# Norm1's row spread by full products, its load on ScalarE's queue, and k's first cast behind h's: the prologue of an encoder block on one core

## The chip, the core and the metric

The kernel runs on one NeuronCore of a Trainium2 chip. The metric is the device time of one execution in microseconds (us). Before the change it is 890.23 us, the median of three runs (890.15, 890.23 and 893.89).

## The reference

One layer of a bidirectional encoder over x of 512 tokens by 1024 channels, all in float32. Cut to what matters here:

```python
h = rmsnorm(x, norm1_w[l])          # y = x * rsqrt(mean(x*x) + eps) * norm1_w
proj = h @ w_in[l]                  # pooling | q | k | v | z | betas, decays | merge gates
# branch A: multi-scale pooling; branch B: conv + SiLU + l2norm on q/k/v, gated delta rule
# forward and backward, gated RMSNorm; merge; output projection; residual
h2 = rmsnorm(x, norm2_w[l])
u = dwconv_centered(h2 @ ffn_up[l], ffn_conv_w[l], ffn_conv_b[l])
x = x + (silu(gate) * val) @ ffn_down[l]
return rmsnorm(x, final_norm_w)
```

The change concerns the first line, `rmsnorm(x, norm1_w)`, and the first two products with `w_in`: the 32 columns of betas and decays (`gate`) and the first 128 columns of k (`k0`).

## The kernel before, in words

Every float32 product with a weight is done as three fp32r products of high and low parts: `mm3` (L370 to L373) multiplies high by high, high by low and low by high. A weight block of 128 columns is loaded by SyncE's queue, its high part is a ScalarE cast (L392), its low part two subtractions on GpSimd (POOL, L396), each over half of the contraction. The activations h are stored transposed, as `h_hi` and `h_lo`.

The order of the work is set by a planner: each task is declared with its engine, an estimated cost, the buffers that it reads and writes and a key; `Planner.run` simulates the engines and, whenever one is free, takes the ready task with the smallest key. The program is then written out in that order, and every engine executes its own part of it in that order. A small key (-9e6) means early; `FEED` (-3e6) is the key of weight loads and casts.

The prologue before the change:

- POOL fills the constants one after another: the identity `ident`, eps tiles, the all-ones tile `ones`, triangular and mask tiles.
- TensorE (PE) does 13 and then 8 transposes of the identity (`pe_warm`, L571 to L574), whose result nobody reads.
- SyncE loads x in four tiles of 128 tokens (x0 to x3), and between x0 and x1 the row `norm1_w`, 1024 numbers in one partition (`load_n1`).
- `spread_n1` (L560 to L565) spreads that row over 128 partitions by two products of a 1x128 row of ones with 1x512 halves of the row, into two PSUM banks `n1b`.
- `norm_transpose` (L503 to L543) is done for each tile of 128 tokens: ScalarE sums the squares (L511) and takes the root (L514), VectorE (DVE) inverts it (L516) and scales the tile in two halves by the root and by `n1b` (L522), PE transposes each half in four 128x128 pieces (L533), ScalarE casts the result to `h_hi` (L537), DVE subtracts to `h_lo` (L541).
- The gate's products (L442 to L445) and k0's (`mm3`) are done in halves of 256 tokens, so that they can begin with x0 and x1.

Of the kernel before, what the change touches and what calls it, by code (L numbers as in the profile page):

```python
# [9 lines left out]
F32 = mybir.dt.float32  # L10
# [4 lines left out]
P = 128  # L15
S = 512
NT = S // P
D = 1024
# [19 lines left out]
class Planner:  # L38
# [14 lines left out]
    def add(self, eng, cost, fn, r=(), w=(), key=0.0, tab=None, kb=0.0, after=(), land=LAND):  # L53
        t = Task()
        t.land = land
        t.i, t.eng, t.cost, t.fn, t.key, t.tab, t.kb = len(self.tasks), eng, cost, fn, key, tab, kb
        t.preds, t.succs, t.news, t.uses = set(), [], [], set()
        for names, writes in ((r, False), (w, True)):
            for name in names:
                base = name.split("#")[0]  # L60
                known = self.parts.setdefault(base, {})
                ring = base.split(":")[0]
                if ring in self.rings and base not in t.news:
                    t.news.append(base)
                if base not in self.owner:
                    self.owner[base] = t.i
                    if ring in self.rings:
                        self.order[ring].append(base)
                t.uses.add(base)
                hit = list(known) if name == base else [n for n in (base, name) if n in known]  # L70
                for n in hit:
                    wr, rd = known[n]
                    if wr is not None:
                        t.preds.add(wr)
                    if writes:
                        t.preds.update(rd)
                if name == base and writes:
                    known.clear()
                wr, rd = known.get(name, (None, ()))
                known[name] = (t.i, ()) if writes else (wr, rd + (t.i,))  # L80
        t.preds.discard(t.i)
        for b in after:
            t.preds.update(self.users.get(b, ()))
        for b in t.uses:
            self.users.setdefault(b, []).append(t.i)
        self.tasks.append(t)
# [101 lines left out]
def ca(n):  # L188
    return 0.22 + n * 0.00082
# [6 lines left out]
def cp(n):  # L196
    return 0.17 + n * 0.0023
# [12 lines left out]
def hybrid_block(  # L210
# [23 lines left out]
    pe, act, dve, pool, sp = nc.tensor, nc.scalar, nc.vector, nc.gpsimd, nc.sync  # L234
# [16 lines left out]
    def with_table(tab, fn):  # L251
        def run():
            if table["now"] != tab:
                table["now"] = tab
                if TABLES[tab]:
                    act.preload_act_table_set(TABLES[tab])
            fn()

        return run

    def A(cost, fn, r=(), w=(), key=0.0, tab=None):
        add("act", cost, with_table(tab, fn) if tab else fn, r, w, key, tab)

    def V(cost, fn, r=(), w=(), key=0.0):
        add("dve", cost, fn, r, w, key)

    def G(cost, fn, r=(), w=(), key=0.0):
        add("pool", cost, fn, r, w, key)

    def M(cost, fn, r=(), w=(), key=0.0):  # L270
        add("pe", cost, fn, r, w, key)

    def L(kb, fn, r=(), w=(), key=0.0, after=(), land=Planner.LAND, issue=Planner.ISSUE, eng="sp"):
        add(eng, issue, fn, r, w, key, kb=kb, after=after, land=land)
# [6 lines left out]
    FEED, EVICT, CHAIN = -3e6, -2e6, -1e6  # L281

    def f32(ap):
        return ap.bitcast(F32)

    def bank(tag, name):
        return psum.tile([P, 512], F32, tag=tag, bufs=RINGS[tag], name=name)

    def banks2(name, shape=(P, 2, 512)):
        return psum.tile(list(shape), F32, tag="oo", bufs=RINGS["oo"], name=name)  # L290

    stacks = {}
    pools = {}
# [11 lines left out]
    ident = const.tile([P, P], F32, name="ident")  # L305
# [7 lines left out]
    qeps_t = const.tile([P, 1], F32, name="qeps_t")  # L313
    pool.memset(qeps_t, float(P) * EPS * L2_EPS)
    ones = const.tile([P, P], F32, name="ones")
    pool.memset(ones, 1.0)
    ones_r = const.tile([P, P], F32R, name="ones_r")
    tri = const.tile([P, 2, P], F32, name="tri")

# [40 lines left out]
    def ring(pool_name, tag, shape, dt, name):  # L360
        return pools[pool_name].tile(list(shape), dt, tag=tag, bufs=RINGS[tag], name=name)
# [15 lines left out]
    def next_unit():  # L377
        unit["n"] += 1
        return unit["n"] * 100.0

    def weights(src, kt, n, name, u):

        b = {}

        def load():
            b["raw"] = wpool.tile([P, kt, n], F32, tag="wraw", bufs=RINGS["raw"], name=f"wr_{name}")
            sp.dma_start(b["raw"], src)

        def hi():
            b["hi"] = wpool.tile([P, kt, n], F32R, tag="whi", bufs=RINGS["whi"], name=f"wh_{name}")  # L390
            b["lo"] = wpool.tile([P, kt, n], F32R, tag="wlo", bufs=RINGS["wlo"], name=f"wl_{name}")
            act.copy(b["hi"], b["raw"])  # L392

        def lo(i):
            sl = slice(i * kt // 2, (i + 1) * kt // 2)
            pool.tensor_tensor(out=b["lo"][:, sl], in0=b["raw"][:, sl], in1=f32(b["hi"][:, sl]), op=ALU.subtract)  # L396

        whi, wlo = f"whi:{name}", f"wlo:{name}"
        L(kt * n * P * 4 / 1024, load, w=[f"raw:{name}"], key=FEED + u)
        A(ca(kt * n), hi, r=[f"raw:{name}"], w=[whi, f"{wlo}#0"], key=FEED + u)  # L400
        for i in range(2):
            G(cp(kt * n / 2), lambda i=i: lo(i), r=[f"raw:{name}", whi], w=[f"{wlo}#{i}"], key=FEED + u)
        return b, whi, wlo

    def job(src, kt, xs, xr, name, halves=False, pair=False):
# [6 lines left out]
        if pair:  # L412
            def load():
                box["raw"] = wpool.tile([P, kt, n], F32, tag="wraw", bufs=RINGS["raw"], name=f"wr_{name}")
                sp.dma_start(box["raw"], src)

            def split():
                w = box["hi"] = wpool.tile([P, kt, 2 * n], F32R, tag="whi", bufs=RINGS["whi"], name=f"wp_{name}")
                act.copy(w[:, :, 0:n], box["raw"])

            def split2():
                w = box["hi"]
                pool.tensor_tensor(out=w[:, :, n:], in0=box["raw"], in1=f32(w[:, :, 0:n]), op=ALU.subtract)

            whi = f"whi:{name}"
            wlo = whi
            L(128, load, w=[f"raw:{name}"], key=FEED + u)
            A(ca(kt * n), split, r=[f"raw:{name}"], w=[whi], key=FEED + u)
            G(cp(kt * n), split2, r=[f"raw:{name}"], w=[whi], key=FEED + u)
        else:  # L430
            wb, whi, wlo = weights(src, kt, n, name, u)
# [121 lines left out]
    xin = [None] * NT  # L553
    n1 = {}

    def load_n1():
        n1["row"] = pools["st"].tile([1, D], F32, name="n1row")
        sp.dma_start(n1["row"], norm1_w)

    def spread_n1():  # L560
        n1["bc"] = banks2("n1b")
        for hf in range(2):
            pe.matmul(
                n1["bc"][:, hf, :], ones[0:1, :], n1["row"][:, hf * 512 : (hf + 1) * 512], start=True, stop=True
            )  # L565

    def load_x(t):
        xin[t] = pools["st"].tile([P, D], F32, name=f"x1_{t}")
        sp.dma_start(xin[t], xt[t * P : (t + 1) * P, :])

    def pe_warm(n):  # L571
        pt = bank("ds", f"pt_warm{n}")
        for i in range(n):
            pe.transpose(pt[:, 0:P], ident, ident)  # L574

    def hx(k):
        return h_hi[:, k, :], h_lo[:, k, :]
# [819 lines left out]
        L(256, lambda: sp.dma_start(g_scr["m1"][c], b["t"]), r=[f"y:lgp{c}"], w=[f"gscrm1{c}"], key=u - 300)  # L1397


    M(2.6, lambda: pe_warm(13), w=["ds:warm0"], key=-9e6)  # L1400
    A(1.3, lambda: act.preload_act_table_set("sqrt_and_others"), key=-9e6)
    for t, k in ((0, -9e6), (1, -8.9e6), (2, FEED + 240), (3, FEED + 250)):
        L(512, lambda t=t: load_x(t), w=[f"st:x{t}"], key=k)
    L(4, load_n1, w=["st:n1"], key=-8.95e6)
    M(2.0, spread_n1, r=["st:n1"], w=["oo:n1"], key=-8.9e6)
    M(1.6, lambda: pe_warm(8), w=["ds:warm1"], key=-8.8e6)
    for t in range(NT):
        norm_transpose(
            -8e6 + t, lambda t=t: xin[t], [f"st:x{t}"], lambda: [lambda: n1["bc"][:, 0, :], lambda: n1["bc"][:, 1, :]], ["oo:n1", "oo:n1"],
            lambda: h_hi, lambda: h_lo, "h", t,  # L1410
            lambda t=t: ring("st", "xs", (P, D), F32, f"xs_{t}"), f"xs:{t}", f"a{t}", None,
        )
# [108 lines left out]
    for t in range(NT):  # L1521
        L(512, lambda t=t: sp.dma_start(x2[t], xt[t * P : (t + 1) * P, :]), r=["pool:xp"], w=[f"xr{t}#0", f"xr{t}#1"],
          key=unit["n"] * 100, after=[f"pp:do{1 + t}"])
    L(512, lambda: sp.dma_start(pools["n2b"], norm2_w[0].partition_broadcast(P)), r=["pool:xp"], w=["n2b"],
      key=unit["n"] * 100, after=["pp:do5"])
# [48 lines left out]
    for i, (t, hf) in enumerate(order):  # L1574
        u = next_unit()
# [113 lines left out]
    for c in range(NF):  # L1689
        b = {}  # L1690
        for j in range(2):
            c0 = j * FFN + c * P
            box, pp, u = job(ffn_up[0][:, c0 : c0 + P], KD, hx2, hr2, f"up{c}_{j}", halves=c == 0)
# [273 lines left out]
```

## Time and profile before

| | |
|---|---|
| median of three runs | 890.23 us |
| the profiled execution, its own time | 891.73 us |
| span of the profiled execution | 890.0 us |
| busy: PE / PE's weight loads | 877.3 / 738.6 us |
| busy: DVE / ACT / POOL | 547.9 / 461.3 / 497.4 us |
| granted TensorE clock, mean of the run | 0.999 |

Read it from the top: one engine is busy almost throughout, the others are not; so the question for any change is whether it makes PE start earlier, wait less or do less. "PEld" is PE's weight load, which overlaps with its products. SP is SyncE, whose DMA queue carries most loads; ACT is ScalarE; POOL is GpSimd. A plain fp32 product appears as two records in the trace, a transpose as one.

### The profile page before, as it was taken

The page shows a single profiled execution, that of the slowest core. Times are in us where ns is not written, and L with a number is a line of the kernel's source. Part 1 is how long each engine was busy: PE and PEld are TensorE (multiplying, and loading weights), DVE is VectorE, ACT ScalarE, POOL GpSimd, SP SyncE. Part 2 cuts the span into 40 slices and gives each one's busy share as a digit, 9 for nine tenths or more (in the row PEclk, how much of TensorE's full clock was granted, in tenths as well). Part 3 has the DMA queues.
Part 4 walks back from the last instruction along what each step waited for, and adds up shares of the span by engine and source line. Part 5 has one row for each costly group of instructions (what it writes and reads, how often), then busy time and mean ns, then how long its engine had stood idle before and what let it go on. Part 6 is the DMA issues. An engine that isn't in the chain of part 4 may idle for free.

```text
span 890.0 us, 14085 instructions
## 1 busy us (share of the span) xinstructions
PE 877.3 (99%) x5178; PEld 738.6 (83%) x5178; DVE 547.9 (62%) x980; ACT 461.3 (52%) x791; POOL 497.4 (56%) x447
## 2 busy tenths in 40 slices
PE   8999999999999999999999999999999999999997
PEld 6988888798888887888788888888888888888886
DVE  4758686247795976654434243655655554569996
ACT  6589633417868344344844333444443333465664
POOL 3444455225366554253577905777878774567763
PEclk9999999999999999999999999999999999999999
DMA  7265448415255467112798605566766653366554
GB/s 203 78 208 143 124 119 185 102 37 142 60 166 131 119 167 119 31 48 83 250 312 266 193 20 202 200 216 217 240 214 201 234 167 98 116 192 199 167 170 161
DMA packets 176265, 140.20 MB, mean 158 GB/s; under 512 B 32110, under 2 KB 143547, under 8 KB 176196
## 3 DMA queue, kind: packets, MB, share of 16 engines
q1 hardware_dynamic: 167300, 137.20, 50.7%
q10 hardware_dynamic: 8896, 2.10, 1.6%
q8 instruction: 41, 0.67, 0.3%
q14 instruction: 28, 0.23, 0.1%
HBM read 114.08 MB, written 25.20 MB: 156 GB/s over the span
## 4 chain that ended last, share of the span: by engine, by line
PE 96%; DVE 2%; ACT 1%; issue 0%; POOL 0%; DVEq 0%; ACTq 0%; POOLq 0%
PE ps_up L372 9%; PE ps_up L373 9%; PE ps_up L371 9%; PE dn L371 4%; PE dn L372 4%; PE dn L373 4%; PE ps_k L371 2%; PE pw L1139 2%; PE o L1176 2%; PE ps_gp L371 2%; PE ps_k L372 2%; PE ps_k L373 2%; PE ps_wo L372 2%; PE ps_wo L371 2%; PE ps_wo L373 2%; PE ps_gp L372 2%
## 5 line engine op out<-in xcount | busy, mean ns | idle before, releaser
L396 POOL TENSOR_TENSOR wl_up<-wr_up,wh_up 128x512 fp32r<-128x512 f32 x88 | 114.2, 1319 | 53.2 <-ACT wh_up L392 51.0
L372 PE MATMUL ps_up<-h_lo,wh_up 128*128 128x512 f32 (+1 forms) x368 | 139.9, 380 | 0.3 <-DVE h_lo L541 0.3
L371 PE MATMUL ps_up<-h_hi,wh_up 128*128 128x512 f32 (+1 forms) x368 | 140.0, 380 | 0.0
L373 PE MATMUL ps_up<-h_hi,wl_up 128*128 128x512 f32 (+1 forms) x368 | 139.8, 380 | 0.0
L1680 DVE SCALAR_TENSOR_TENSOR c<-ps_up,fw,c 128x511 f32<-128x511 f32 x88 | 66.0, 750 | 101.6 <-ACT c L1674 99.8
L1665 POOL TENSOR_TENSOR tp<-tp 128x512 f32<-128x512 f32 x44 | 60.1, 1366 | 40.0 <-DMA tp<-in_ffn_down_dram 32.0
L1869 POOL TENSOR_TENSOR w_dn<-wr_dn,w_dn 128x512 fp32r<-128x512 f32 x44 | 65.5, 1503 | 29.1 <-ACT w_dn L1866 27.6
L372 PEld LDWEIGHTS ps_up<-h_lo,wh_up 128*128 128x128 f32 x368 | 69.2, 188 | 13.5 <-DVE h_lo L541 0.5
L371 PEld LDWEIGHTS ps_up<-h_hi,wh_up 128*128 128x128 f32 x368 | 69.2, 188 | 13.3
L373 PEld LDWEIGHTS ps_up<-h_hi,wl_up 128*128 128x128 f32 x368 | 69.2, 188 | 13.1
L392 ACT CAST wh_up<-wr_up 128x1024 fp32r<-128x1024 f32 x44 | 46.2, 1051 | 63.8 <-issue 25.5
L1866 ACT CAST w_dn<-wr_dn 128x512 fp32r<-128x512 f32 x69 | 42.4, 621 | 29.5 <-PE dn L373 21.1
L372 PE MATMUL dn<-w_dn,as 128*128 128x512 f32 x141 | 54.2, 385 | 0.0
L373 PE MATMUL dn<-w_dn,as 128*128 128x512 f32 x141 | 54.2, 385 | 0.0
L371 PE MATMUL dn<-w_dn,as 128*128 128x512 f32 x141 | 54.2, 385 | 0.0
L1634 DVE TENSOR_TENSOR as<-a,as 128x512 fp32r<-128x512 f32 (+1 forms) x41 | 42.8, 1069 | 0.1
L396 POOL TENSOR_TENSOR wl_k<-wr_k,wh_k 128x512 fp32r<-128x512 f32 x16 | 20.1, 1281 | 32.8 <-ACT wh_k L392 17.0
L1630 ACT CAST as<-a 128x512 fp32r<-128x512 f32 (+1 forms) x41 | 21.5, 534 | 32.3 <-DVE a L1701 28.6
L396 POOL TENSOR_TENSOR wl_v<-wr_v,wh_v 128x512 fp32r<-128x512 f32 x16 | 20.4, 1294 | 27.7 <-ACT wh_v L392 27.7
L1674 ACT ACTIVATE c<-ps_up,fw 128x512 f32<-128x512 f32 x44 | 33.9, 770 | 0.0
L396 POOL TENSOR_TENSOR wl_z<-wr_z,wh_z 128x512 fp32r<-128x512 f32 x16 | 20.4, 1295 | 22.8 <-ACT wh_z L392 22.8
L396 POOL TENSOR_TENSOR wl_gp<-wr_gp,wh_gp 128x512 fp32r<-128x512 f32 x16 | 21.5, 1364 | 19.6 <-ACT wh_gp L392 18.0
(361 smaller groups left out, 2438.2 us busy)
## 6 DMA issues: line engine op xcount, KB each, us to landing
wr_up<-in_ffn_up_dram SPq DMA_DIRECT2D x44, 512.0 KB, 3.8
tp<-in_ffn_down_dram SPq DMA_DIRECT2D x22, 512.0 KB, 5.2
t_scr<-tp SPq DMA_DIRECT2D x44, 256.0 KB, 2.5
wr_dn<-t_scr SPq DMA_DIRECT2D x20, 512.0 KB, 3.7
wr_dn<-in_ffn_down_dram SPq DMA_DIRECT2D x15, 512.0 KB, 3.6
x<-in_x_dram SPq DMA_DIRECT2D x8, 512.0 KB, 5.4
wr_k<-in_w_in_dram SPq DMA_DIRECT2D x8, 512.0 KB, 5.8
wr_z<-in_w_in_dram SPq DMA_DIRECT2D x8, 512.0 KB, 4.0
```

What stands on the lines that cost most here:

```text
L371: pe.matmul(ps, ahi, bhi, start=first, stop=False)
L372: pe.matmul(ps, ahi, blo, start=False, stop=False)
L373: pe.matmul(ps, alo, bhi, start=False, stop=last)
L392: act.copy(b["hi"], b["raw"])
L396: pool.tensor_tensor(out=b["lo"][:, sl], in0=b["raw"][:, sl], in1=f32(b["hi"][:, sl]), op=ALU.subtract)
L1630: act.copy(sets[p][:, i : i + n, 0, :], src())
L1634: dve.tensor_tensor(out=w[:, :, 1, :], in0=src(), in1=f32(w[:, :, 0, :]), op=ALU.subtract)
L1665: G(cp(512), lambda o=o, x=x, y=y: pool.tensor_tensor(out=w(*o), in0=w(*x), in1=w(*y), op=ALU.subtract), r=[n(*x), n(*y)], w=[n(*o)], key=u)
L1674: act.activation(b[j], box["ps"], AF.Identity, scale=fw[:, 1, ci : ci + 1], bias=fw[:, 3, ci : ci + 1])
L1680: dve.scalar_tensor_tensor(out=y[:, lo:hi], in0=box["ps"][:, lo + sh : hi + sh], scalar=fw[:, k, ci : ci + 1], in1=y[:, lo:hi], op0=ALU.mu ...
L1866: act.copy(b["w"][:, 0, :], raw["t"][:, j, :])
L1869: eng.tensor_tensor(out=b["w"][:, 1, :], in0=raw["t"][:, j, :], in1=f32(b["w"][:, 0, :]), op=ALU.subtract)
```

## The change

- `ones` is filled by VectorE instead of POOL.
- The row of norm1 gets a tile of 128 partitions that VectorE clears; the row is loaded into its first partition by ScalarE's queue, and the spread is a full product with the 128x128 tile of ones. The two halves are two tasks; their waits are declared apart.
- The warming is eight plain products of `ones` with itself, ahead of the spread, and three behind it, in place of 13 and 8 transposes ahead of it.
- k0's cast is declared to come behind the four casts of h of the first two token tiles, with a key among norm1's. The statistics of x2 are declared to come behind the two casts of x1's tile.

```diff
-    pool.memset(ones, 1.0)
+    dve.memset(ones, 1.0)
...
+        first = [f"h#hi{t}{hf}" for t in range(2) for hf in range(2)] if name == "k0" else []
-        A(ca(kt * n), hi, r=[f"raw:{name}"], w=[whi, f"{wlo}#0"], key=FEED + u)
+        A(ca(kt * n), hi, r=[f"raw:{name}", *first], w=[whi, f"{wlo}#0"], key=-8e6 + 1.5 if first else FEED + u)
...
+    def clear_n1():
+        n1["row"] = pools["st"].tile([P, D], F32, name="n1row")
+        dve.memset(n1["row"], 0.0)
+
     def load_n1():
-        n1["row"] = pools["st"].tile([1, D], F32, name="n1row")
-        sp.dma_start(n1["row"], norm1_w)
-
-    def spread_n1():
-        n1["bc"] = banks2("n1b")
-        for hf in range(2):
-            pe.matmul(
-                n1["bc"][:, hf, :], ones[0:1, :], n1["row"][:, hf * 512 : (hf + 1) * 512], start=True, stop=True
-            )
+        act.dma_start(n1["row"][0:1, :], norm1_w)
+
+    def spread_n1(hf):
+
+        if hf == 0:
+            n1["bc"] = banks2("n1b")
+        pe.matmul(n1["bc"][:, hf, :], ones, n1["row"][:, hf * 512 : (hf + 1) * 512], start=True, stop=True)
...
-            pe.transpose(pt[:, 0:P], ident, ident)
+            pe.matmul(pt[:, 0:P], ones, ones, start=True, stop=True)
...
-    M(2.6, lambda: pe_warm(13), w=["ds:warm0"], key=-9e6)
+    M(3.3, lambda: pe_warm(8), w=["ds:warm0"], key=-9e6)
...
-    L(4, load_n1, w=["st:n1"], key=-8.95e6)
-    M(2.0, spread_n1, r=["st:n1"], w=["oo:n1"], key=-8.9e6)
-    M(1.6, lambda: pe_warm(8), w=["ds:warm1"], key=-8.8e6)
+    V(0.6, clear_n1, w=["st:n1"], key=-9.5e6)
+    L(0, load_n1, w=["st:n1"], key=-8.95e6, eng="act")
+    for hf in range(2):
+        M(1.0, lambda hf=hf: spread_n1(hf), r=["st:n1"], w=[f"oo:n1#{hf}"], key=-8.9e6)
+    M(0.7, lambda: pe_warm(3), r=["oo:n1"], w=["ds:warm1"], key=-8.8e6)
     for t in range(NT):
         norm_transpose(
-            -8e6 + t, lambda t=t: xin[t], [f"st:x{t}"], lambda: [lambda: n1["bc"][:, 0, :], lambda: n1["bc"][:, 1, :]], ["oo:n1", "oo:n1"],
+            -8e6 + t, lambda t=t: xin[t], [f"st:x{t}", *(["h#hi10", "h#hi11"] if t == 2 else [])], lambda: [lambda: n1["bc"][:, 0, :], lambda: n1["bc"][:, 1, :]], ["oo:n1#0", "oo:n1#1"],
```

What stands in a row on PE, from the program's first product to the gate's first, before (the lines are those of the kernel before; `pt_warm` is the warming, `n1b` the spread row, `pt_a` a transposed half of x):

```order
L574 MATMUL pt_warm_156<-ident 128x128 x13
L574 MATMUL pt_warm_215<-ident 128x128 x8
L563 MATMUL n1b<-n1row,ones 128x512 x2
L533 MATMUL pt_a_0_256<-ident,xs_233 128x128 x4
L533 MATMUL pt_a_1_267<-ident,xs_233 128x128 x4
```

and now:

```order
L578 MATMUL pt_warm_156<-ones 128x128 x8
L569 MATMUL n1b<-n1row,ones 128x512 x2
L578 MATMUL pt_warm_231<-ones 128x128 x3
L535 MATMUL pt_a_0_245<-ident,xs_223 128x128 x4
L535 MATMUL pt_a_1_255<-ident,xs_223 128x128 x4
```

Ten products fewer stand ahead of the first transposes of x, and three of the warming ones have moved behind the spread.

ScalarE from its first instruction to the statistics of x2, before (`wp_gate` is the gate's weight, `wh_k` k0's high part, `h_hi` a cast of h, `xs_292` the square sum of x2):

```order
L1401 ACT_TABLE_LOAD
L1419 CAST ones_r<-ones 128x128
L511 ACTIVATE xs_233,nst_a_234<-x_0_171 128x1024
L514 ACTIVATE nst_a_234<-nst_a_234,eps_t 128x1
L511 ACTIVATE xs_245,nst_a_246<-x_1_201 128x1024
L514 ACTIVATE nst_a_246<-nst_a_246,eps_t 128x1
L419 CAST wp_gate<-wr_gate 128x8x32
L392 CAST wh_k_263<-wr_k_209 128x1024
L537 CAST h_hi<-pt_a_0_256 128x4x128
L537 CAST h_hi<-pt_a_1_267 128x4x128
L537 CAST h_hi<-pt_a_0_277 128x4x128
L511 ACTIVATE xs_292,nst_a_293<-x_2_213 128x1024
```

and now:

```order
L1405 ACT_TABLE_LOAD
L563 DMA n1row<-in_norm_w_dram 1x1024
L1425 CAST ones_r<-ones 128x128
...
L421 CAST wp_gate<-wr_gate 128x8x32
L539 CAST h_hi<-pt_a_0_245 128x4x128
L539 CAST h_hi<-pt_a_1_255 128x4x128
L539 CAST h_hi<-pt_a_0_265 128x4x128
L539 CAST h_hi<-pt_a_1_273 128x4x128
L392 CAST wh_k_280<-wr_k_201 128x1024
L513 ACTIVATE xs_291,nst_a_292<-x_2_207 128x1024
```

k0's cast has moved behind all four casts of h, x2's square sum behind both, and the row's load stands between the table load and the first cast.

On PE the gate's first half was cut by three groups of k0's products (`ps_k`); now it stands in one piece ahead of them:

```order
L444 MATMUL ps_gate<-h_hi,wp_gate 64x256
L445 MATMUL ps_gate<-h_lo,wp_gate 32x256 x2
L447 MATMUL ps_gate<-h_hi,wp_gate 64x256
L371 MATMUL ps_k_312<-h_hi,wh_k_280 128x256
L372 MATMUL ps_k_312<-h_lo,wh_k_280 128x256
L373 MATMUL ps_k_312<-h_hi,wl_k_281 128x256
```

The same 16 products of the gate and the same eight groups of k0 stand ahead of the gate's second half, in another order. From there on the rows of every engine are those of before.

## Rows read from the trace of the kernel before

**Rows 1.** The page of the profile: busy time, share of the span and instructions of each engine, and the engines' shares of the chain of work that ended last.

```profile
PE 877.3 (99%) x5178; PEld 738.6 (83%) x5178; DVE 547.9 (62%) x980; ACT 461.3 (52%) x791; POOL 497.4 (56%) x447
...
PE 96%; DVE 2%; ACT 1%; issue 0%; POOL 0%; DVEq 0%; ACTq 0%; POOLq 0%
```

**Rows 2.** The table by stretches, its first three: the stretch and its length in us, busy us (and instructions) of PE, PEld, DVE, ACT and POOL, granted TensorE clock, share of the DMA engines, GB/s.

```profile
0.00:12.50 12.50, 9.94 (x32) 7.03 (x33) 2.51 (x6) 6.13 (x11) 6.93 (x52) 1.00 0.92 273
12.50:25.00 12.50, 12.17 (x96) 11.23 (x95) 8.62 (x15) 8.00 (x19) 1.50 (x3) 1.00 0.38 94
25.00:50.00 25.00, 25.00 (x154) 22.04 (x153) 17.42 (x38) 17.14 (x38) 11.55 (x10) 1.00 0.32 88
```

**Rows 3.** Whom PE waited for in the whole span: us in total, times, longest.

```profile
PE l1a L962 <- ACT nm L1028: 1.4, 1, 1.4
PE pt_v L778 <- ACT cv_v L763: 1.3, 1, 1.3
```

**Rows 4.** The chain of work that ended last, from 0 to 30 us, in order of time: start us, us, what.

```profile
6.37 3.72 PE n1b L563 x4
...
10.12 0.76 DVE xs L522
...
11.01 2.81 PE pt_a L533 x12
...
15.20 0.31 PE ps_gate L443
15.51 0.11 PE ps_gate L442
15.62 0.12 PE ps_gate L443
...
18.54 0.44 PE pt_a L533 x4
...
22.33 0.12 PE ps_gate L442
...
27.05 1.01 PE pt_gate L607 x8
```

**Rows 5.** The timeline from 0 to 26 us: start us, us, engine, line, operation, out<-in, count, and in brackets the idle time before and what ended it.

```profile
0.80 1.28 ACT L1401 ACT_TABLE_LOAD   x1 [0.80 <-PEq L1954]
...
1.04 0.20 POOL L316 MEMSET ones<- 128x128 f32 x1
1.26 0.32 SPq L558 DMA_DIRECT2D n1row<-in_norm_w_dram  x1
...
1.63 4.74 PE L574 MATMUL pt_warm<-ident 128*128 128x128 f32 x21 [1.63 <-POOL ident masks.py:199]
...
4.44 1.06 ACT L511 ACTIVATE xs<-x 128x1024 f32<-128x1024 f32 x1 [2.05 <-DMA x<-in_x_dram]
...
5.95 0.16 DVE L516 RECIPROCAL nst_a<-nst_a 128x1 f32<-128x1 f32 x1 [5.95 <-ACT nst_a L514]
...
8.42 1.04 ACT L392 CAST wh_k<-wr_k 128x1024 fp32r<-128x1024 f32 x1 [0.77 <-DMA wr_k<-in_w_in_dram]
9.54 2.49 POOL L396 TENSOR_TENSOR wl_k<-wr_k,wh_k 128x512 fp32r<-128x512 f32 x2 [1.09 <-ACT wh_k L392]
...
10.12 1.41 DVE L522 SCALAR_TENSOR_TENSOR xs<-x,nst_a,n1b 128x512 f32<-128x512 f32 x2 [4.00 <-PE n1b L563]
...
14.32 1.06 ACT L511 ACTIVATE xs<-x 128x1024 f32<-128x1024 f32 x1
14.46 0.69 DVE L541 TENSOR_TENSOR h_lo<-pt_a,h_hi 128x512 fp32r<-128x512 f32 x1 [0.16 <-ACT h_hi L537]
...
15.37 0.58 ACT L537 CAST h_hi<-pt_a 128x512 fp32r<-128x512 f32 x1
```

**Rows 6.** Records of PE by tile and line: duration in ns, least, median and greatest, then the first and last start in us and the form. The first is the warming, the second the spread of norm1, the others the transposes of x around 11 to 12, 13.7 to 14.5 and 17.6 to 18.3 us.

```profile
L574 PE MATMUL pt_warm<-ident x21: 421/421/476, 1.6 to 5.9; 128*128 128x128 f32 x21
...
L563 PE MATMUL n1b<-n1row,ones x4: 1056/1056/1217, 6.3 to 9.0; 1*128 1x512 f32 x4
...
L533 PE MATMUL pt_a<-ident,xs x5: 421/421/448, 11.0 to 11.9; 128*128 128x128 f32 x5
...
L533 PE MATMUL pt_a<-ident,xs x5: 273/421/472, 13.4 to 14.4; 128*128 128x128 f32 x5
...
L533 PE MATMUL pt_a<-ident,xs x4: 272/272/303, 17.7 to 18.0; 128*128 128x128 f32 x4
```

**Rows 7.** Two copies on DVE, the largest and one of the smallest: the first from the table of groups (busy us, mean ns of one, idle before), the second from the instructions on the tile `pg` (ns least, median, greatest).

```profile
L917 DVE COPY rev<-un 128x1024 f32<-128x1024 f32 x2 | 2.4, 1220 | 1.0 <-ACT inv L915 1.0
...
L665 DVE COPY g_all<-pg x2: 180/180/181, 45.0 to 45.0; 128x32 f32<-128x32 f32 x2
```

**Rows 8.** From the longest pieces of the chain over the whole span: eight records of plain fp32 products (the product with the state S) in a row.

```profile
210.70 0.89 PE ks L1115 x8
```

**Rows 9.** DMA issues: out<-in, queue, count, KB each, median us from issue to landing.

```profile
gp_scr<-sgp SPq DMA_DIRECT2D x8, 256.0 KB, 2.0
...
ea<-in_a_log_dram SPq DMA_DIRECT2D x1, 8.0 KB, 3.1
dtb<-in_dt_bias_dram SPq DMA_DIRECT2D x1, 8.0 KB, 2.7
```

## The prediction

> **What bounds the kernel now.** I read the page first: its busy line and the shares of the chain that ended last [rows 1]. TensorE is busy for 877.3 of 890.0 us, and PE holds 96% of the chain. Time can therefore be won only where PE stands still or does work that nobody needs. The table by stretches [rows 2] shows where that is: of the first 12.5 us PE is busy for 9.94, of the next 12.5 for 12.17, and from 25 us on it is full. The list of who waited for whom has few entries that matter later; the two longest of PE behind the prologue are 1.4 and 1.3 us [rows 3], in other stages.
>
> So the chain through the prologue [rows 4] is the thing to read. PE warms from 1.63 to 6.37 us (21 transposes [rows 5]), spreads norm1's row from 6.37 to 10.09 (four records), and VectorE's first scaling starts at 10.12. That scaling had its reciprocal long before: at 5.95 to 6.11 [rows 5]. Hence VectorE stands still for 4.0 us, and what ends last there is the spread of norm1. From 15.20 on PE follows itself without a hole that counts: the second half of the gate starts at 22.33, the gate's transposition at 27.05 [rows 4].
>
> Two more readings. First, TensorE's speed: the granted clock reads 1.00 throughout [rows 2], but the records of one 128x128 transpose take 421 ns in the warming and again at 11 to 12 us, 273 in the fastest record of those around 13.7 to 14.5, and 272 at 17.6 [rows 6]. [...] In steady order a transpose takes 4.74 / 21 = 0.226 us at the lower level and 0.44 / 4 = 0.110 at the upper [rows 4]. Second, the order of the instructions: before and after differ on every engine only in the first rows; from the first cast behind the second gate half on they stand alike. Whatever the prologue wins or loses is handed on as a shift of the whole rest.
>
> **The change, part by part.** T is the start of the first scaling, 10.12 before.
>
> *Start of the warming.* PE waited until 1.63 for POOL's identity. Now it waits for VectorE's memset of `ones`. Engines begin at 0.80; POOL's memset of that tile took 0.20 [rows 5]. VectorE's memset is not in the trace: its copies take 0.18 (128x32) and 1.22 (128x1024) [rows 7]. I take 0.25, nearest the row of the same tile; PE starts at 1.1, between 1.0 and 2.0.
>
> *Eight products for thirteen transposes ahead of the row.* A plain fp32 product leaves two records (the spread: 2 products, 4 records). Sixteen records at the lower level, each priced like a transpose, are 16 x 0.226 = 3.6 us; at the upper, by the products on S, 0.89 / 8 = 0.111 each [rows 8], 1.8. I take 3.6, since nothing ran before: end at 4.7.
>
> *The row's load on ScalarE's queue.* It stands behind the table load, which ends at 2.08 [rows 5], and behind the clearing of the 128x1024 tile (up to 1.22 [rows 7], so by 2.3). Issue at 2.2. Landing took 2.0 us for the quickest transfer of the trace, 3.1 and 2.7 for the two of 8 KB; the row itself, issued at 1.26, was in by 6.3 when PE took it right behind the warming, so at most 5.04 [rows 5, 6, 9]. I take 2.9, by the 8 KB rows: 5.1, bounds 4.2 and 7.3. On ScalarE the issue hides in its idle time up to 4.44; SyncE loses one issue of 0.32, so x1 and what follows come that much earlier, which no one waits for.
>
> *The spread by full products.* It starts at 5.1. At the lower level the one-row products took 3.72 us [rows 4]; at the upper I halve that, as the transposes halve: 1.86. [...] No run here shows a full product of 512 columns, and I price it no shorter. What raises the level? In the trace it rose once, while only transposes had run for some 3 us, and it did not rise under 4.74 us of transposes followed by 3.72 us of one-row products. Here 3.6 us of full products stand ahead. I take the first record at the lower level and three at the upper: 0.93 + 1.40 = 2.3, bounds 1.86 and 3.72. Both halves must be done before the first scaling, as before (its one wait covers both). T becomes 7.5.
>
> *Three warming products behind the spread.* They lie in the wait for the first scaling (0.76 from 10.12 [rows 4]) and cost 3 x 2 x 0.111 = 0.7 at the upper level: hidden.
>
> *From T to the gate.* VectorE needs four scalings and three residues one after the other; before that was 10.12 to 15.16, and PE's gate ran from 15.20. The transposes are faster but VectorE still ends last: T + 5.0. No change.
>
> *k's cast behind h's.* Before, k's cast ran at 8.42 and POOL's residue at 9.54, in dead time [rows 5]. Now the cast (1.04) comes behind the fourth h cast. That one needs transposes which wait for a buffer until VectorE's first residue (T + 3.5), and then four transposes (0.44), a hand-over of 0.25 and its own 0.58: T + 4.9. So k's cast ends at T + 5.9 and POOL's first half (1.25) ends at T + 7.3. The gate's first half, now all in one piece, is 16 x 0.115 = 1.84 us and covers T + 4.95 to T + 6.8; two of k's products bring 7.05, so PE stands 0.25 us. On ScalarE x2's square sum (1.06), which before ran at 14.32 = T + 4.2, comes behind the cast at T + 5.9. In return the fourth h cast no longer waits for it (it began at 15.37 before [rows 5]). From square sum to reciprocal x0 took 4.44 to 6.11, 1.67 us, so x2's first scaling (0.76) ends at T + 8.4, and PE, which needs it ahead of k's third group, stands 0.25 more. x3's sum follows at T + 7.4, its reciprocal at T + 9.1, its two scalings (1.41) end at T + 10.6, and three residues of 0.67 behind them at T + 12.6. The gate's second half needs the third: T + 12.65, against 22.33 = T + 12.2 before. Loss: 0.45. POOL's masks, cut apart by one place, are wanted tens of us later.
>
> **Sum.** (10.12 - 7.5) - 0.45 = 2.2 us earlier at the gate's second half, and so at the end. The profiled execution took 891.73 (span 890.0, 1.7 around it), so 889.5 on its scale. It stands 1.5 above the median of the three runs (890.15, 890.23, 893.89), so 888.1 by the median. The spread between runs may itself be the level: 1.86 us lie between a norm1 spread at either level, and a run of before in which it rose earlier would have less to win. For that I add 0.2: **888.3 us**.
>
> **Rivals.**
>
> 1. *The gain shrinks to half a microsecond or nothing.* Either the row lands near 7.3, or the full products stay at the lower level (T = 8.9), or before's usual run had its spread at the upper level already. For it: the spread between runs, and the large loads that fill the DMA engines while the row comes. Against: 8 KB in 3 us. The mid case is (10.12 - 8.9) - 0.45 = 0.8: 889.4. With the row at 7.3 the spread at the upper level gives T = 9.2 and 889.8, at the lower T = 11.0 and 891.6. Chance 0.30.
>
> 2. *Slower: the gate and k at half speed.* Before, transposes at the lower level kept PE busy from 11.01 on [rows 4], and the level rose just ahead of the gate. Now, if the level rises early, PE has between T and T + 5 only 16 transposes of 0.11 and three products, 2.4 of 5 us. If the level falls there, the stretch that follows (22.33 - 15.20 = 7.13 us of products) runs at half rate until it rises again. [...] The longest run at the lower level in the trace is 1.63 to 14.4 [rows 6], 12.8 us: a loss of up to 6.4, 4.2 net; half of it gives 891.2, all of it 894.4. Against: before, the level rose while nothing but transposes ran. [...] Chance 0.08, centre 892.
>
> 3. *More than forecast.* The level rises within the eight products and the row is there at 4.7: T = 6.6, gain 3.1, 887.2. It can't go far below: with the reciprocal at 6.11 T is never under 6.1, a gain of 4.0 less 0.45. Chance 0.12.
>
> **How the numbers follow.** The forecast holds 0.50 within about 0.8 us. The range must leave out 2 in 10: from 886.5 (rival 3 with a run's spread) to 890.7 (rival 1 but for its latest end, not rival 2). About 0.5%, 4.45 us, is what a measurement of this kernel can tell from no change. The whole stall at stake is 4.0 us, so only a before and after drawn from opposite ends of the runs' spread could show faster by more: 0.06. Slower by more needs rival 2 at its far end: 0.03. The rest, 0.91, is within.
>
> **What would show it.** In the profile after: warming from 1.1; n1row's products at 5 us with records near 1056 ns at first and near 600 later; the first scaling at 7 to 8; gate products from 12 to 13 at 0.115 each; k's third product waiting for POOL's residue; the gate's second half near 20.2. Wrong would be: records of 1056 ns to the end of the spread, PE waiting for the row's DMA beyond 6, or gate products at twice their spacing.

## The result and the profile after

The changed kernel takes 892.24 us (median of 14 runs, 890.31 to 893.82); the kernel before, beside it, 890.14 (14 runs, 889.17 to 893.89). The ratio is 1.0020, 95% interval 1.0011 to 1.0029: 1.8 us slower (a ratio here takes in all runs of both kernels, so it need not be the quotient of the two medians, which lie 2.1 apart). That is less than 0.5%, but on the other side of the forecast (888.3) and outside its range (to 890.7). The profiled execution of after took 892.21 us, a usual run of it; its span is 890.5, half a microsecond over the one of before.

The page's busy line and chain shares, and the stretches (columns as in [rows 1, 2]):

```profile
PE 876.8 (98%) x5179; PEld 738.6 (83%) x5179; DVE 551.2 (62%) x982; ACT 460.8 (52%) x791; POOL 496.5 (56%) x446
...
PE 94%; DVE 2%; ACT 1%; DMA 1%; SPq 1%; issue 0%; DVEq 0%; ACTq 0%
```

```profile
0.00:12.50 12.50, 9.76 (x32) 7.44 (x33) 3.39 (x8) 4.71 (x10) 4.29 (x49) 1.00 0.92 271
12.50:25.00 12.50, 11.34 (x93) 10.42 (x92) 8.76 (x16) 8.58 (x18) 3.58 (x4) 1.00 0.37 96
25.00:50.00 25.00, 25.00 (x155) 22.11 (x155) 16.21 (x37) 17.28 (x38) 11.67 (x10) 1.00 0.31 88
```

In the first 25 us PE is busy for 21.10 us where [rows 2] have 22.11, and from 25 us on it is full again: it stands still 1.0 us longer. The timeline shows where (columns as in [rows 5]):

```profile
0.90 0.17 DVE L316 MEMSET ones<- 128x128 f32 x1 [0.90 <-PEq L1960]
...
1.12 3.78 PE L578 MATMUL pt_warm<-ones 128*128 128x128 f32 x16 [1.12 <-DVE ones L316]
1.22 0.91 DVE L560 MEMSET n1row<- 128x1024 f32 x1 [0.16 <-issue]
...
2.17 0.53 ACTq L563 DMA_DIRECT2D n1row<-in_norm_w_dram  x1
...
6.52 3.75 PE L569 MATMUL n1b<-n1row,ones 128*128 128x512 f32 x4 [1.62 <-DVE nst_a L518]
...
10.07 1.49 PE L578 MATMUL pt_warm<-ones 128*128 128x128 f32 x6
...
10.31 1.41 DVE L524 SCALAR_TENSOR_TENSOR xs<-x,nst_a,n1b 128x512 f32<-128x512 f32 x2 [3.89 <-PE n1b L569]
...
15.06 1.05 ACT L392 CAST wh_k<-wr_k 128x1024 fp32r<-128x1024 f32 x1
15.09 0.31 PE L445 MATMUL ps_gate<-h_lo,wp_gate 128*32 128x256 f32 x1 [0.42 <-DVE h_lo L543]
...
16.20 2.54 POOL L396 TENSOR_TENSOR wl_k<-wr_k,wh_k 128x512 fp32r<-128x512 f32 x2 [7.26 <-ACT wh_k L392]
```

The warming ends at 4.90, and PE stands until 6.52: 1.62 us. The name in that bracket misleads: VectorE's reciprocal ran at 6.25, but the spread reads only `ones` and the row. In the profile of after without the k edits (below) the bracket at the same place names the row's DMA. Then the spread takes 3.75 us, as long as the four records of before, 3.72 [rows 4]. The first scaling, T, is at 10.31 instead of 10.12. Two rows by tile (least, median and greatest ns, as in [rows 6]) and the waits of PE (total, times, longest):

```profile
L569 PE MATMUL n1b<-n1row,ones x4: 1061/1061/1193, 6.5 to 9.2; 128*128 128x512 f32 x4
...
L611 PE MATMUL pt_gate<-eye,gate_rows x8: 272/273/293, 27.4 to 28.2; 64*128 64x32 f32 x8
```

```profile
PE n1b L569 <- DVE nst_a L518: 1.6, 1, 1.6
PE l1a L966 <- ACT nm L1032: 1.4, 1, 1.4
PE pt_v L782 <- ACT cv_v L767: 1.3, 1, 1.3
```

The spread's records are at the lower level throughout: 1061 ns, where those of before take 1056 [rows 6]. A level is here no more than one of the two durations that records of one form show: 1052 to 1061 ns or 587 to 592 at the median for the spread's in the profiles of this case, 421 or 271 to 273 for a transpose. The chain has the gate's second half from 22.78 and its transposition from 27.50 (start us, us, what, as in [rows 4]):

```profile
22.78 0.12 PE ps_gate L444
...
27.50 1.01 PE pt_gate L611 x8
```

Against 27.05 [rows 4] the transposition is 0.45 us later, nearly all of the half microsecond in the span.

### The profile page after: what moved, and what is told of

It is laid out like the page before. It is cut to its first block, busy times and chain, and to the rows that moved or that the text cites. A ratio compares the mean times of both kernels' runs of the same rounds, so it can differ in the third digit from the quotient of the medians.

```text
span 890.5 us, 14090 instructions
## 1 busy us (share of the span) xinstructions
PE 876.8 (98%) x5179; PEld 738.6 (83%) x5179; DVE 551.2 (62%) x982; ACT 460.8 (52%) x791; POOL 496.5 (56%) x446
## 4 chain that ended last, share of the span: by engine, by line
PE 94%; DVE 2%; ACT 1%; DMA 1%; SPq 1%; issue 0%; DVEq 0%; ACTq 0%
PE ps_up L372 9%; PE ps_up L371 9%; PE ps_up L373 9%; PE dn L373 4%; PE dn L371 4%; PE dn L372 4%; PE ps_k L371 2%; PE ps_k L373 2%; PE pw L1143 2%; PE o L1180 2%; PE ps_gp L371 2%; PE ps_wo L373 2%; PE ps_wo L372 2%; PE ps_k L372 2%; PE ps_wo L371 2%; PE ps_gp L373 2%
```

## The experiments

"Usual before" below is the profile of `b_again`. Times are medians beside the kernel before on the same chip. Theory L: the level of PE during the spread decides, and the usual run of before already has the upper one.

**b_again: the kernel before, unchanged.**

> The kernel before, unchanged, profiled and timed once more. Theory L (TensorE's level): a usual run of before, near 890.1 us, has norm1's spread at the upper level, because 21 transposes run up to it without a gap; only its dearer runs (891 to 894) have it at the lower one, as the profiled run of 891.73 had. So if this profile comes from a run of 889 to 890.5 us, its four spread records last about 600 ns (not 1056) and the first scaling starts near 8.3 us (not 10.1); if from a run above 891, 1056 ns again. Rival K (the order of k's cast and x2's statistics costs the whole 2 us) and rival D (the difference lies in a later stage) expect 1056 ns and 10.1 us in either case. Ratio 1.000 for all.

890.12 us, ratio 0.9996 (0.9987 to 1.0005); the profiled run took 889.93. Timeline, two pieces of the chain, records by tile (pt_a in two stretches: 9 to 11 and 11 to 13 us) and the first two stretches:

```profile
1.63 4.64 PE L574 MATMUL pt_warm<-ident 128*128 128x128 f32 x21 [1.63 <-POOL ident masks.py:199]
...
8.22 1.41 DVE L522 SCALAR_TENSOR_TENSOR xs<-x,nst_a,n1b 128x512 f32<-128x512 f32 x2 [2.12 <-PE n1b L563]
```

```profile
6.27 1.92 PE n1b L563 x4
...
24.98 1.00 PE pt_gate L607 x8
```

```profile
L574 PE MATMUL pt_warm<-ident x21: 324/421/473, 1.6 to 5.9; 128*128 128x128 f32 x21
...
L563 PE MATMUL n1b<-n1row,ones x4: 587/587/692, 6.2 to 7.6; 1*128 1x512 f32 x4
...
L533 PE MATMUL pt_a<-ident,xs x10: 273/421/448, 9.1 to 10.9; 128*128 128x128 f32 x10
...
L533 PE MATMUL pt_a<-ident,xs x8: 421/421/473, 10.7 to 12.5; 128*128 128x128 f32 x8
...
L607 PE MATMUL pt_gate<-eye,gate_rows x8: 272/273/293, 24.9 to 25.7; 64*128 64x32 f32 x8
```

```profile
0.00:12.50 12.50, 9.86 (x41) 7.57 (x42) 4.38 (x9) 7.67 (x14) 6.95 (x52) 0.88 0.90 273
12.50:25.00 12.50, 12.45 (x103) 11.67 (x102) 6.69 (x12) 7.66 (x18) 2.82 (x5) 0.99 0.40 100
```

The level rose within the 21 transposes: the quickest of them takes 324 ns, and the spread's records 587 instead of 1056. T is 8.22, 1.90 before the T of the run that the prediction was built on. The span is 888.2, 1.8 shorter. So one program has two prologues, and the forecast was made from the longer one. Theory L holds: of the five profiles here that have 21 transposes ahead of the spread (before, b_again, b_kcast, a_t21, b_swap) only before's has the spread at the lower level (1056 ns at the median; the others 587, 588, 592 and 588).

**b_kcast: before, with the edits to k's cast and x2's statistics alone.**

```diff
-        A(ca(kt * n), hi, r=[f"raw:{name}"], w=[whi, f"{wlo}#0"], key=FEED + u)
+        first = [f"h#hi{t}{hf}" for t in range(2) for hf in range(2)] if name == "k0" else []
+        A(ca(kt * n), hi, r=[f"raw:{name}", *first], w=[whi, f"{wlo}#0"], key=-8e6 + 1.5 if first else FEED + u)
...
-            -8e6 + t, lambda t=t: xin[t], [f"st:x{t}"], ...
+            -8e6 + t, lambda t=t: xin[t], [f"st:x{t}", *(["h#hi10", "h#hi11"] if t == 2 else [])], ...
```

> The kernel before with one part of the change alone: k0's first cast and x2's statistics behind the casts of h. Theory L: only the 0.45 us that PE loses between the first scaling and the gate's second half, so about +0.45 us (ratio 1.0005). Rival K: this part carries the slowdown, +2 us (1.0023). Rival D: nothing, 1.000.

891.19 us, ratio 1.0004 (0.9993 to 1.0015). Timeline and chain:

```profile
8.48 1.41 DVE L523 SCALAR_TENSOR_TENSOR xs<-x,nst_a,n1b 128x512 f32<-128x512 f32 x2 [2.46 <-PE n1b L564]
```

```profile
25.93 1.00 PE pt_gate L608 x8
```

T is 8.48 and the gate's transposition 25.93: 17.45 us apart, against 16.76 in usual before (24.98 - 8.22). The edits cost 0.69 us there; in the time this is inside the interval.

**a_nokcast: after, without those edits.** (The same diff taken back.)

> The changed kernel with k0's cast and x2's statistics put back where they were; the spread, the row's queue and the warming stay changed. Theory L: the loss that stays is the spread at the lower level behind a wait for the row, +1.65 us over before (ratio 1.0018), the spread's records 1061 ns. Rival K: back to before, 1.000. Rival D: 1.0023 or 1.000 depending on which edit reaches the later stage, with the gate's second half no later than in before.

892.32 us, ratio 1.0019 (1.0007 to 1.0032). Without the k edits after is as slow as with them, so most of the loss lies in the spread's part: T is 10.30 and the gate's transposition 27.02, 2.04 later than in usual before. They are 16.72 apart; with the edits 17.19: the edits cost 0.47 here. The profiled run took 893.81, 1.5 above this kernel's median, and it waits 1.4 us for a load of `ext` near 160 us, of which more at c_first. The chain of this kernel (start us, us, what) and PE's row name what PE waited for:

```profile
2.17 4.25 DMA n1row<-in_norm_w_dram
6.55 3.73 PE n1b L568 x4
...
27.02 1.00 PE pt_gate L610 x8
```

```profile
6.55 3.71 PE L568 MATMUL n1b<-n1row,ones 128*128 128x512 f32 x4 [1.66 <-DMA n1row<-in_norm_w_dram]
```

**a_warm12: after, with 12 warming products ahead of the spread.**

```diff
-    M(3.3, lambda: pe_warm(8), w=["ds:warm0"], key=-9e6)
+    M(5.7, lambda: pe_warm(12), w=["ds:warm0"], key=-9e6)
```

> The changed kernel with twelve warming products ahead of the spread in place of eight, so that PE has no gap between warming (to about 6.8 us) and the spread (row in at about 6.5). Theory L, if a gapless stretch of products raises the level as the 21 transposes do in usual runs: records of the spread near 600 ns, first scaling near 8.7, time about 0.3 to 0.9 us over before (1.0003 to 1.001), i.e. 1.2 to 1.8 less than the change. If products of ones don't raise the level: 1061 ns, first scaling near 10.7, 892.6 us. Rivals K and D: no gain on the change, 892.2 to 892.6.

891.28 us, ratio 1.0010 (0.9998 to 1.0023). PE works from 1.12 to 6.22 and waits 0.38 for the row, which lands no sooner; but the spread is at the upper level, 592 ns a record:

```profile
6.60 1.96 PE L569 MATMUL n1b<-n1row,ones 128*128 128x512 f32 x4 [0.38 <-DMA n1row<-in_norm_w_dram]
...
8.60 0.75 DVE L524 SCALAR_TENSOR_TENSOR xs<-x,nst_a,n1b 128x512 f32<-128x512 f32 x1 [2.27 <-PE n1b L569]
```

Four products that nobody reads bring T forward by 1.71 us. About 1 us of that reaches the median; in the profile PE loses 0.8 later, waiting for a load of `ext` (see c_first).

**a_t21: after, with 21 transposes of the identity ahead of the spread.**

```diff
-            pe.matmul(pt[:, 0:P], ones, ones, start=True, stop=True)
+            if n == 21:
+                pe.transpose(pt[:, 0:P], ident, ident)
+            else:
+                pe.matmul(pt[:, 0:P], ones, ones, start=True, stop=True)
...
-    M(3.3, lambda: pe_warm(8), w=["ds:warm0"], key=-9e6)
+    M(4.6, lambda: pe_warm(21), w=["ds:warm0"], key=-9e6)
```

> The kernel after, with 21 transposes of the identity ahead of the spread in place of its 8 products of ones (the three products behind it stay). Theory L: the level rises under transposes as it rose in the run of before, at about 5.9 us, and the spread from 6.4 to 6.5 us on runs at the upper level (records near 590 ns): first scaling near 8.5 instead of 10.3, time about 890.7, ratio to before 1.000 to 1.001. [...]

891.01 us, ratio 1.0008 (0.9998 to 1.0018). Behind 21 transposes the spread is at the upper level, as it is behind the 12 products of a_warm12:

```profile
L569 PE MATMUL n1b<-n1row,ones x4: 592/592/857, 6.5 to 8.1; 128*128 128x512 f32 x4
```

T is 8.69 and the gate's transposition at 25.87, 1.63 before after's; the span, 888.9, is 1.6 shorter. So with the row on ScalarE's queue, the full products and the k edits all kept, and the spread starting at 6.51 as after's does at 6.52, its records of 592 ns in place of 1061 give that back. The row also tells what full products are worth by themselves: 592 ns a record, one-row products 587, both at the upper level.

**b_t8: before, with 8 transposes and no second warming; b_t8act: the same, the row on ScalarE's queue.**

```diff
-    M(2.6, lambda: pe_warm(13), w=["ds:warm0"], key=-9e6)
+    M(1.6, lambda: pe_warm(8), w=["ds:warm0"], key=-9e6)
...
-    M(1.6, lambda: pe_warm(8), w=["ds:warm1"], key=-8.8e6)
```

and in b_t8act besides:

```diff
-        sp.dma_start(n1["row"], norm1_w)
+        act.dma_start(n1["row"], norm1_w)
-    L(4, load_n1, w=["st:n1"], key=-8.95e6)
+    L(0, load_n1, w=["st:n1"], key=-8.95e6, eng="act")
```

> Before, with 8 transposes of the identity ahead of the spread instead of 21 (the other 13 are left out). It shows when the row is in on SyncE's queue, and what level PE has without a long warming. Theory L (the level of PE during the spread makes the difference; the row is in well before 6.3 us on SyncE's queue): PE is done with the transposes at 1.63 + 8 x 0.226 = 3.4, takes the row when it lands, between 3.4 and 6.3 (issued at 1.26, the 8 KB loads took 3), and has records near 1056 ns: spread of 3.7 us, first scaling at 7.1 to 10, in the middle 8.2. Theory Q (the queue makes the difference: on SyncE's queue the row is never late): the same landing, below 4.5, and first scaling near 8.2. Rival R (the row lands after 6 us on any queue, since the large loads fill the engines): PE stands still until 6 to 6.5 and the first scaling is near 10, as in the kernel after.

> The same with the row loaded into its one partition by ScalarE's queue, right behind the table load (about 2.1 us), with no clearing ahead of it. Beside the run on SyncE's queue it prices the queue alone. Theory Q: landing 4.2 us after issue as in the kernel after, so near 6.4 us, and the spread begins there; SyncE's row has been in 2 us or more earlier. Rival R (no difference between queues beyond the later issue of 0.9 us): the landing is about 0.9 us later than on SyncE's queue.

One run each: 891.79 and 892.26 us. First the timeline of b_t8, then of b_t8act:

```profile
1.26 0.32 SPq L558 DMA_DIRECT2D n1row<-in_norm_w_dram  x1
...
4.10 3.78 PE L563 MATMUL n1b<-n1row,ones 1*128 1x512 f32 x4 [0.50 <-DMA n1row<-in_norm_w_dram]
...
13.22 0.41 PE L442 MATMUL ps_gate<-h_hi,wp_gate 128*64 128x256 f32 x1
```

```profile
0.83 0.53 ACTq L558 DMA_DIRECT2D n1row<-in_norm_w_dram  x1
...
3.53 3.78 PE L563 MATMUL n1b<-n1row,ones 1*128 1x512 f32 x4
```

On SyncE's queue the row is in by 4.10, 2.84 us after its issue. On ScalarE's the issue stands not behind the table load but beside it, at 0.83, and the row is in by 3.53. So the queue is not slow, and theory Q falls. The row's load takes at most 2.7 us when issued at 0.83, 2.84 at 1.26 and 4.25 at 2.17. The later it is issued, the more loads of x and of weights stand ahead of it; that these are the reason is likely, but no run changes them alone. My text for b_t8act had the issue at 2.1, which was wrong: in after it was the wait for VectorE's clearing that held it until then.

These two show a second thing. T is 7.91 in b_t8 and 7.34 in b_t8act, earlier than in usual before, and yet they end later: the gate's first products are 0.41 us records at the lower level where usual before has 0.28, and its transposition starts 0.5 and 1.3 us later than there (at 25.52 and 26.29 in the chains). In these two, then, warming that seemed hidden had paid for the gate; in c_first, with ten transposes, the gate's first two records take 0.30 and 0.31. They also lost 1.3 and 0.6 us in the wait for `ext` (see c_first). The spread itself is slow in both, 1056 ns a record, though in b_t8act nothing but eight transposes and no pause worth listing stand ahead of it.

**c_first: before, with the row first on SyncE's queue, 6 transposes ahead of the spread and 4 behind.**

```diff
-    M(2.6, lambda: pe_warm(13), w=["ds:warm0"], key=-9e6)
+    M(1.2, lambda: pe_warm(6), w=["ds:warm0"], key=-9e6)
...
-    L(4, load_n1, w=["st:n1"], key=-8.95e6)
+    L(4, load_n1, w=["st:n1"], key=-9.1e6)
...
-    M(1.6, lambda: pe_warm(8), w=["ds:warm1"], key=-8.8e6)
+    M(0.8, lambda: pe_warm(4), r=["oo:n1"], w=["ds:warm1"], key=-8.8e6)
```

> Before, with the row's load first on SyncE's queue (ahead of x0), 6 transposes ahead of the spread and 4 behind it (11 fewer in all); the spread remains that of one row. Theory: the row, first in an empty queue, is in by 3 to 3.5 us, PE spreads it from 3.3 to 7.0 even at the lower level, x0 comes 0.3 to 0.4 later, so its reciprocal is there at 6.3 to 6.5 and the first scaling begins near 7.1 instead of 8.2 (run of before with the spread at the upper level). If the gate runs at the upper level, that is 1.1 us earlier to the end: about 889.0 against 890.1, ratio 0.9988. Rival 1: with 10 transposes instead of 21 the level is still low at the gate (12 us), and the gate and k lose what was won: ratio 1.000 to 1.002. Rival 2: the row lands near 6 also here; the first scaling is near 9.8 and the time 891.7, ratio 1.0018.

890.80 us, ratio 1.0010 (0.9998 to 1.0021). The prologue went as expected:

```profile
3.11 3.77 PE L563 MATMUL n1b<-n1row,ones 1*128 1x512 f32 x4
...
6.92 1.40 DVE L522 SCALAR_TENSOR_TENSOR xs<-x,nst_a,n1b 128x512 f32<-128x512 f32 x2 [0.27 <-PE n1b L563]
```

T is 6.92, 1.30 before usual before, with the spread at the lower level (1052 ns); but the k cast now falls between two casts of h. PE's first product of z is at 43.7 us against 44.3 in usual before: 0.6 won. The chain shows where that goes:

```profile
141.04 4.79 DMA e_scr<-rev
...
149.06 8.47 DMA ext<-e_scr
157.58 0.43 PE l1a L962 x26
```

PE waits 0.94 us for a load of `ext`, at the end of a store and a load that took 13 us between them. It is tempting to say that PE now comes too early for a chain that was just in time. The traces say otherwise. The store is issued 0.60 us earlier too (141.04 against 141.64 in usual before), and the wait is not one of early kernels alone; the longest is a_nokcast's, whose PE comes to z at 46.7, 2.4 us after usual before:

```profile
PE l1a L965 <- DMA ext<-e_scr: 1.4, 1, 1.4
```

What goes with the wait is how long the load of `ext` takes from issue to landing: 7.7 to 8.6 us in the seven profiles that have it (a_nokcast, a_warm12, b_t8, b_t8act, c_first, c_again, c_kcast), 6.7 to 7.3 in the five that have not (before, b_again, b_kcast, after, a_t21).

**c_again: the same kernel again. c_kcast: with the k edits of b_kcast added.**

> The kernel with the row first on SyncE's queue a second time, unchanged, beside the others on one chip: its eleven times went from 889.1 to 893.9. Theory E: a second profile without the wait for ext has a span near 887.7 (888.6 less 0.9), and one with it near 888.6; the median is 890.3 to 890.8 as before. Rival: the first profile's wait was an exception, and the median comes out near 889.5.

> The kernel with the row first on SyncE's queue, with the change's edits to k's first cast and to x2's statistics added. Without them the cast of k (1.05 us) stands between the first and the second cast of h, and the gate's stream begins 5.4 us after the first scaling instead of 5.0. Theory: the gate begins 0.4 to 0.9 us earlier (near 11.6 to 11.9 us), but k's residue on POOL comes 2 us later, as in before with these edits alone, which were 0.4 us later at the gate's transposition: first product of ps_z near 43.7 to 44.1 us, time within 0.4 us of the kernel without them. Rival: the loss of 0.45 that the prediction put on these edits came from x2's statistics behind the cast, and it is the whole effect here too: 0.45 us later.

890.01 us, ratio 1.0000 (0.9987 to 1.0013), and 890.05, ratio 0.9991 (0.9980 to 1.0003). Both profiles have the wait, first c_again's, then c_kcast's:

```profile
PE l1a L962 <- DMA ext<-e_scr: 0.6, 1, 0.6
```

```profile
PE l1a L963 <- DMA ext<-e_scr: 1.0, 1, 1.0
```

With c_first that is three of three, with the load at 8.1 to 8.3 us. c_again's median, 890.01, lies between the rival's 889.5 and theory E's 890.3, and its profile has a wait of 0.6 where c_first's has 0.94; so neither text is borne out. The first product of z is at 43.5 and 43.7 us: with the row early, the k edits cost 0.2 at most. c_kcast beats after by 2.2 us; against before it is not told from no change.

**b_swap and c_swap: before and c_first with the stores to e_scr ahead of those to u_scr.**

```diff
-        for n, rows, scr, d in (("inv", hi_, "u", 1), ("inv", lo_, "e", 0), ("rev", lo_, "u", 0), ("rev", hi_, "e", 1)):
+        for n, rows, scr, d in (("inv", lo_, "e", 0), ("inv", hi_, "u", 1), ("rev", hi_, "e", 1), ("rev", lo_, "u", 0)):
```

> Before, with the two stores to e_scr put ahead of those to u_scr on SyncE's queue (the planner then also sets some later loads and casts in another order). It prices this edit alone, for the next run. Theory E (what PE waits for at its first l1a near 157 us, where it waits at all, is the chain of store to e_scr and load of ext): the stores are issued 0.5 us earlier and the wait becomes rarer; in a run of before without that wait nothing changes. About 890.0, ratio 0.999 to 1.001. Rival U: nm, loaded from u_scr 0.6 us later, takes ext's place, and PE waits for it: up to 0.6 us longer, 890.7.

> The kernel with the row first on SyncE's queue, with the same swap. In the profile without the swap PE comes to its first product of ps_z 0.6 us earlier than in the run of before with its spread at the upper level, and then waits 0.94 us for ext near 157 us. Theory E: without that wait it ends 0.6 to 1.0 us before the swapped before: about 889.2, ratio to before 0.999. Rival U: PE waits there for nm instead, and the time stays at 890.3 to 890.8.

895.06 us, ratio 1.0039 (1.0022 to 1.0056), and 892.27, ratio 1.0019 (1.0007 to 1.0031). Both miss. The wait for ext is gone from both profiles, but the planner moved loads and casts far beyond the swap, and a wait for ScalarE's `nm` near 350 us grew from 1.4 to 2.2 us. The stretch from 340 to 360 us of b_swap, then of c_swap (columns as in [rows 2]):

```profile
340.00:360.00 20.00, 17.64 (x387) 13.20 (x387) 9.37 (x21) 7.61 (x23) 5.70 (x8) 0.74 0.25 69
```

```profile
340.00:360.00 20.00, 17.56 (x430) 13.82 (x417) 11.17 (x25) 8.35 (x25) 4.45 (x7) 0.91 0.20 58
```

In usual before the granted clock there is 1.00. So these two do not decide about theory E: they exchanged one wait for another. Nor do they price the early row: c_swap's median is 2.8 us below b_swap's, but at the first product of z its PE is only 1.0 us ahead (43.9 and 44.9); the rest comes later, where the clock differs too, and b_swap's own runs lie between 891.15 and 896.72.

## Why the prediction was wrong

Three terms of the sum failed: the row's landing, the level of TensorE during the spread, and the before from which the gain was taken off. The first two make T 10.31 where I had 7.5, 2.81 us. The third is 1.3: I took 1.5 off to come from the profiled run to the median and gave back 0.2. The k edits cost less than forecast by 0.2. Together that is the 3.9 us between 888.3 and 892.24.

- **Start of the warming and its eight products: right.** 1.12 for 1.1, ended at 4.90 for 4.7; 16 records in 3.78 us, 0.236 each.
- **The row's landing: mis-sized.** I took 5.1 within 4.2 to 7.3; it came near 6.42 (2.17 + 4.25, from a_nokcast). The 8 KB loads that I went by [rows 9] are issued at 11.07 and 13.12 us, behind the large loads of the start. And I named the table load and the clearing as what holds the issue; only the clearing did (b_t8act).
- **The spread: the level failed.** I took 2.3, three records at the upper level; it was 3.75, all at the lower. Eight products end at 4.90, then PE stands 1.62 us and starts the spread slow, at 1061 ns a record. With 12 products (a_warm12) or 21 transposes (a_t21), and a pause of 0.38 us or less, it is fast, at 592. Whether the missing products or the pause did it no run parts: b_t8act has a short warming, no pause and a slow spread (1056). That a full product is no shorter than a one-row one was my estimate, with no row of before to show it; 592 ns in a_t21 and 587 in b_again bear it out.
- **What before was.** For the case that "a run of before in which it rose earlier would have less to win" I added 0.2 us. It is the usual run, worth 1.90 at T. Of the 35 runs of before beside the last experiments 23 lie between 889.49 and 890.44, as b_again's profiled 889.93 does, and of the 35 beside the first ones 19 lie at or below 890.44; the 891.73 that I calculated with is among the longer runs. A run's time alone does not tell its prologue, though: the wait for `ext` lengthens runs as well. The hint stood in my own text: the profiled run was 1.5 us above the median, and the fast and slow records of this prologue differ by 1.86.
- **T to the gate, and k's cast: right in the main.** The gate's stream starts 4.78 after T (5.0 forecast); k's cast ends at T + 5.80 (5.9); the second half of the gate comes at T + 12.47 (12.65). That is 0.26 behind the before that I went by (22.33 - 10.12 = 12.21), where I forecast 0.45. At the gate's transposition the edits cost 0.47 beside a_nokcast and 0.69 in b_kcast, so that the first of these is so near 0.45 is luck. The three products behind the spread take 1.49 us at the lower level, twice my 0.7, and are hidden all the same.
- **Rivals.** Rival 1 named all three causes but took them as alternatives. The lower level, before's usual run and most of the later landing came true together; its worst sum, 891.6, still left out the second of them. Rival 2 did not happen in after: the gate's products have 0.28 us records at the upper level. In b_t8 and b_t8act a part of it did, and near the half rate that I had only from the transposes [rows 4]: the gate's records start 0.21 us apart there, 0.12 in usual before.

Against usual before the terms add up so: the spread starts 0.25 us later (6.52 and 6.27), takes 1.84 longer to T, and 0.43 more pass from T to the gate's transposition (17.19 and 16.76). That is 2.52 us; the spans differ by 2.3, the profiled times by 2.28, the medians by 2.1. By far the largest term is the level.

Open: why some runs of one kernel get the rise before the spread and others not (587 ns in b_again, 1056 in before's profile), and why the load of `ext` lands 6.7 us after its issue in one profile and 8.6 in another, and in c_first, c_again and c_kcast always near the upper end. Two of after's 14 runs took 890.31 and 890.57, as they would with a fast spread; no profile shows that.

## What to carry to other kernels

- Before costing a change from one profiled run, put its time among the other runs. If it is off by as much as the level of TensorE is worth in that stretch (here 1.90 us at T), it may be another prologue: profile again, and build the sum from a usual run, or carry both.
- Warming is worth what it does to the work right behind it. Count it with the gap that follows: cutting it short to be early was lost in after, where PE then waited 1.62 us for the row and the spread took 3.75 us, against 0.38 and 1.96 us with four products more (a_warm12).
- A small load was early here when it was issued at the very start, on either queue: at 0.81 on SyncE's (c_first) it was in by 3.11, at 0.83 on ScalarE's (b_t8act) by 3.53. And read a gain at the start in the profile, stage by stage, ahead of the median: a later load whose landing differs from one execution to another, here by up to 1.9 us, can hide it.

## What the runs showed of the hardware beside this

- The granted clock of a stretch reads 1.00 over the first 12.5 us of after, where every record of the spread is at the lower level (1061 ns), and 0.88 over those of b_again, where they are at the upper (587). In this prologue the level is read from durations.
- The level falls as well as rises: in b_again the transposes take 273 ns at best near 9 us and all 421 or more from 10.7 to 12.5, behind the one-row spread and a pause of 0.93 us, and 273 again from 15.6.
- In b_swap a wait 0.8 us longer than before's went with a granted clock of 0.74 from 340 to 360 us, where it is 1.00 in usual before; that kernel's median is 4.8 us up. c_swap has as long a wait there (2.3 us) with 0.91, and its median is 2.0 us up: the wait does not fix what the clock does.
